# The output projections' last transposing transfers on ScalarE's queue, and another order of the FFN's raw tiles

## The chip, the cores and the metric

The kernel runs on one core of a Trainium2 chip. The metric is the device time of one execution in microseconds; 2091.7 us is the median of three runs of the kernel before (2091.61 to 2091.89). The core has TensorE (matrix products, called PE in the profile, with its weight loads as PEld), VectorE (DVE), ScalarE (ACT), GpSimd (POOL) and SyncE (SP). SP computes nothing here; its queue issues transfers. ScalarE and GpSimd can issue transfers too, from the same queue as their other instructions, in order.

## The reference

Two decoder layers over a residual stream of 256 positions by 2048 columns, in float32. Each layer mixes, projects, and then runs a gated FFN:

```python
for layer in range(DEPTH):                    # DEPTH = 2
    xn = rms_norm(h, norm_mix[layer])
    if layer % 2 == 0:                        # window attention beside an mLSTM
        mix = swa_mlstm_mixer(xn, w_in_even[j], w_out_even[j], ...)
    else:                                     # forgetting attention
        mix = forgetting_attention_mixer(xn, w_in_odd[j], fox_b_f[j], w_out_odd[j])
    h = h + mix                               # mix ends with a 2048 x 2048 output projection
    h = h + swiglu(rms_norm(h, norm_ffn[layer]), w_gate[layer], w_up[layer], w_down[layer])
return rms_norm(h, norm_final)

def swiglu(xn, w_gate, w_up, w_down):         # hidden width 5632
    return (jax.nn.silu(xn @ w_gate) * (xn @ w_up)) @ w_down
```

## The kernel before

**Products.** Every float32 operand is split into a high part of fewer bits (`hi`, written by ScalarE as a cast, L206 for plain chunks and L380 elsewhere) and the rest (`lo`, a subtraction on VectorE, L207 and L381). A product is three matmuls, hi by hi, hi by lo and lo by hi, summed in PSUM (`three`, L557 to L559; in `gemm` L244 to L246). Weights come in chunks of 256 rows by 512 columns, 512 KB, loaded by the SP queue into raw tiles (L145). Four raw tiles (pool `wr`) serve the plain chunks. The split parts of a plain chunk go into one of six `hi` tiles of the pool `wp`.

**The output projection.** `out_proj` makes the 2048 columns in four blocks `n` of 512, two at a time: blocks 0 and 1, then 2 and 3. When a block is done, VectorE adds it to the residual `h` (`add_out`, L395, one instruction for each half of the positions), ScalarE takes sums of squares for the norm (`square_sum`, L267), and the block has to be turned so that its columns lie on the partitions for the FFN's products. `split_turned` does this with transfers: ScalarE copies the block's two 16-bit planes (L338, two copies), and for each plane and each half of the positions one transposing transfer (L340) moves it, four for a block. SP issues them, in its one queue with the weight loads. A function `join` comes back: ScalarE merges the planes (L345), then scales and splits the result into `xh`, `xl` (L386, L387), and for the mixed pairs makes sums and differences (L326, L294 to L297, into `sx`).

**When the joins run.** The joins of blocks 0 and 1 run inside the second half of the projection. Those of blocks 2 and 3 run in the FFN's first group, at its steps 3 and 5 (`LATER = (6, 10, 3, 5)`, `run_due`), each ordered behind ScalarE's latest cast. Step p of the group needs the columns 256 p to 256 p + 255 of the turned input: steps 0 to 3 those of blocks 0 and 1, steps 4 and 5 those of block 2, steps 6 and 7 those of block 3.

**The FFN's steps.** `pair_group` walks eight steps (`ORDER`: plain at 0, 2, 4, 6 and 7, mixed at 1, 3 and 5). A plain step takes a gate chunk and an up chunk, 24 matmuls. A mixed step makes the same products with seven instead of eight block products, 21 matmuls. It loads both chunks into one raw tile of four pieces from the list `quads`, casts three pieces at once (L380, 128x1536), lets VectorE form differences in place (L645, L648, L649), and casts those into two `hi` tiles (L380, two casts of 128x1024).

**The raw tiles of the mixed steps.** `quads` has three tiles, used in turn. `own` is the sixth tile of `wp`, free when a chunk of the projection is done with. The other two are the slots of the tag `quad` in the FFN's pool; one of them was the room in which block 1 was turned (`scrap`), the other is unused before the FFN. After the projection the other five tiles of `wp` are the `stock` for the FFN's split parts.

**What sets the order.** The kernel's text gives the order of work. A planner goes through it, holds each instruction until by its own estimates its inputs are ready, and so writes one fixed order for each engine's queue; a queue is then worked off strictly in order, an instruction waiting at its head for semaphores. A transfer's issue counts as an instruction of the queue that issues it. `issue_after` puts an instruction behind another one on its engine.

Of the kernel before, what the change touches and what calls it, by code (L numbers as in the profile page):

```python
# [7 lines left out]
F32 = mybir.dt.float32  # L8
# [9 lines left out]
P = 128  # L18
# [5 lines left out]
NB = 512  # L24
CK = 2
# [27 lines left out]
LATER = (6, 10, 3, 5)  # L53
LATER_DOWN = (5, 6)
QUADS = 2
# [13 lines left out]
def mixed_of(order):  # L69
    return [p for w, p in order if w]  # L70
# [5 lines left out]
def trunk(  # L76
# [19 lines left out]
    nc = tc.nc  # L96
# [7 lines left out]
    stock, triples, quads = [], [], []  # L104
# [110 lines left out]
    def new_acc():  # L215
        return two_banks(0, "acc")
# [8 lines left out]
    def gemm(acc, lhs, w, c0, n, k_from, k_to, k_all, skew=1, step=0, halved=False):  # L225
        k0 = k_from
        while k0 < k_to:
            last = k_to == k_all and k0 + skew * CK >= k_all
            chunks = [load_chunk(w, kc, c0, n) for kc in range(k0, k_all if last else k0 + CK, CK)]
            run_due(later, step + k0 // CK)  # L230
            order = [(i, t) for i in range(len(chunks) * CK) for t in range(NT)]
            if last:
                order.sort(key=lambda it: it[1])
            order = [(i, t, slice(0, n)) for i, t in order]
            if last and halved:
                m = CK * (len(chunks) * NT - 1)
                order = order[:m] + [(i, t, slice(a, a + n // 2)) for a in (0, n // 2) for i, t, _ in order[m:]]
            for i, t, cs in order:
                k = k0 + i
                hi, lo = (c[:, i % CK, cs] for c in chunks[i // CK])  # L240
                ah, al = lhs(k)
                ts = slice(t * P, (t + 1) * P)
                o = acc[t][:, cs]
                nc.tensor.matmul(o, ah[:, ts], hi, start=(k == 0), stop=False)  # L244
                nc.tensor.matmul(o, ah[:, ts], lo, start=False, stop=False)  # L245
                nc.tensor.matmul(o, al[:, ts], hi, start=False, stop=(k == k_all - 1 and cs.stop == n))  # L246
            k0 += len(chunks) * CK
# [14 lines left out]
    def square_sum(key, n):  # L262
        if n == 0:
            sums[key] = sm.tile([P, NT, 4], F32, tag="ss", name="ss")
        for t in range(NT):
            junk = junk_of[0].tile([P, NB], BF16, tag=junk_of[1], name="junk", bufs=junk_of[2])
            nc.scalar.activation(  # L267
                junk, h[:, t, n * NB : (n + 1) * NB], AF.Square, accum_out=sums[key][:, t, n : n + 1]
            )
# [34 lines left out]
    def split_scaled(idx, n, extra=None, joined=None):  # L304
        both = two_banks(1, "pt") if joined is None else None
        for half in range(2):
            if joined is None:
                pt = both[half].rearrange("p (i t q) -> p i t q", i=2, t=NT)
                for i in range(2):
                    k = 4 * n + 2 * half + i  # L310
                    for t in range(NT):
                        nc.tensor.transpose(pt[:, i, t, :], h[:, t, k * P : (k + 1) * P], ident)
            else:
                pt = joined[:, 2 * half : 2 * half + 2, :].rearrange("p i (t q) -> p i t q", t=NT)
            for i in range(2):
                k = 4 * n + 2 * half + i
                src = pt[:, i, :, :].rearrange("p t q -> p (t q)")
                split_gained(xh[:, k, :], xl[:, k, :], src, idx * KT + k)
            pair = 2 * n + half
            if extra is not None and (pair in mixed_of(ORDER) or pair == FOURTH):  # L320
                sh, sl, x4, pool = extra

                def copies(full):
                    for i in range(2):
                        g = gT[:, idx * KT + 2 * pair + i : idx * KT + 2 * pair + i + 1]
                        nc.scalar.mul(full[:, i, :], pt[:, i, :, :].rearrange("p t q -> p (t q)"), g)  # L326

                if pair == FOURTH:
                    sums_of(pool, rooms(xh), rooms(xl), copies, x4=x4)
                else:  # L330
                    j = mixed_of(ORDER).index(pair)
                    sums_of(pool, sh[:, j, :, :], sl[:, j, :, :], copies)

    def split_turned(idx, n, flat, turned, extra=None):
        planes = flat.bitcast(U16).rearrange("p (b t n) -> p b t n", b=2, t=NT)
        hu = h[:, :, n * NB : (n + 1) * NB].bitcast(U16).rearrange("p t (n b) -> p t n b", b=2)
        for b in range(2):
            nc.scalar.copy(planes[:, b, :, :], hu[:, :, :, b])  # L338
            for t in range(NT):
                nc.sync.dma_start_transpose(turned[:, b, :, t, :], planes[:, b, t, :])  # L340

        def join():
            ju = flat.bitcast(U16).rearrange("p (n b) -> p n b", b=2)
            for b in range(2):
                nc.scalar.copy(ju[:, :, b], turned[:, b, :, :, :].rearrange("p k t q -> p (k t q)"))  # L345
            split_scaled(idx, n, extra, flat.rearrange("p (k s) -> p k s", k=4))

        return join
# [18 lines left out]
    def scrap(fp, n):  # L367
        if n % 2 == 0:
            box = fp.tile([P, 4, NB], F32, tag="c", name="box", bufs=1)
            halves = box[:, 0:2, :], box[:, 2:4, :]  # L370
        elif n == 3:
            halves = [fp.tile([P, 3, NB], F32, tag=f"sd{i}", name="box", bufs=1)[:, 0:CK, :] for i in range(2)]
        else:
            box = fp.tile([P, 2 * CK, NB], F32, tag="quad", name="box", bufs=QUADS)
            halves = box[:, 0:2, :], box[:, 2:4, :]
        flat, turned = (a.rearrange("p a n -> p (a n)") for a in halves)
        return flat, turned.bitcast(U16).rearrange("p (b k t q) -> p b k t q", b=2, t=NT, q=P)
# [14 lines left out]
    def add_out(acc, n):  # L392
        for t in range(NT):
            o = h[:, t, n * NB : (n + 1) * NB]
            nc.vector.tensor_tensor(out=o, in0=acc[t], in1=o, op=ALU.add)  # L395
# [139 lines left out]
    def out_proj(w, idx, key, extra):  # L535
        last, rest = KT - 4, []
        for n0 in (0, 2):
            accs = [new_acc() for _ in range(2)]
            for i in range(2):
                gemm(accs[i], m_of, w, (n0 + i) * NB, NB, 0, last, KT, step=6 * i)  # L540
            for i in range(2):
                gemm(accs[i], m_of, w, (n0 + i) * NB, NB, last, KT, KT, step=6)
                add_out(accs[i], n0 + i)
                (later if n0 == 0 else rest).append(
                    (LATER[n0 + i], split_turned(idx, n0 + i, *scrap(extra[3], n0 + i), extra))
                )
                square_sum(key, n0 + i)
        return rest
# [247 lines left out]
    def close_layer(layer, w_out, idx, key, **rest):  # L796
        with tc.tile_pool(name=f"fp{layer}", bufs=2) as fp:
            junk_of[:] = fp, "tmp", 2
            nx = len(mixed_of(ORDER))
            nd = max(len(mixed_of(o)) for o in DOWN.values())  # L800
            sx = [fp.tile([P, nx, 4, P], F32R, name=f"sx{i}", bufs=1) for i in range(2)]
            x4 = fp.tile([P, 2, P], F32R, name="x4", bufs=1)
            todo = out_proj(w_out, idx, key, (*sx, x4, fp))
            sd = [fp.tile([P, nd, 4, P], F32R, tag=f"sd{i}", name=f"sd{i}", bufs=1) for i in range(2)]
            triples.extend([fp.tile([P, 3, NB], F32R, name=f"{a}{i}", bufs=1) for a in ("hi", "lo")] for i in range(2))
            stock.extend([slot() for _ in range(5)])
            own = wp.tile([P, 2, CK, NB], F32R, tag="hi", name="raw").rearrange("p a k n -> p (a k) n").bitcast(F32)
            quads.extend([own] + [fp.tile([P, 2 * CK, NB], F32, tag="quad", name="raw", bufs=QUADS) for _ in range(QUADS)])
            ffn(layer, fp, sx, x4, sd, key, todo, **rest)
            stock.clear()  # L810
            triples.clear()
            quads.clear()
# [380 lines left out]
    with tc.tile_pool(name="od", bufs=1) as od:  # L1193
# [80 lines left out]
        for i in range(4):  # L1274
# [23 lines left out]
            elif i < 3:  # L1298
                n = NB if i == 1 else VT
                vs.append(nat1(project(wi1, c_v + (i + 1) * NB, n), n, "vn", bufs=2))  # L1300

            def v_of(j, b, i=i, vn=vs[i]):
# [6 lines left out]
                lambda j, b, qt=qt: qt[:, j, b * P : (b + 1) * P],  # L1309
# [10 lines left out]
                turned=i in (0, 2),  # L1320
# [11 lines left out]
    def finish(acc, n, gf):  # L1332
        for t in range(NT):
# [31 lines left out]
            nc.scalar.dma_start(ov[:, t, NB : 2 * NB], b1)  # L1365

    close_layer(1, w_out_odd[0], 3, "f1", finish=finish)


# [47 lines left out]
```

## Time and profile before

| | |
|---|---|
| median of three runs | 2091.7 us |
| profiled execution, its own time | 2090.63 us |
| span of its instructions | 2088.8 us |
| granted TensorE clock over the span | 0.998 |
| TensorE busy | 2072.2 us |
| VectorE busy | 1806.2 us |
| ScalarE busy | 1368.3 us |
| transposing transfers of `split_turned` | 36, all issued by SP |
| output projection ends, FFN starts on TensorE | 323.1 us (layer 0), 1388.2 us (layer 1) |

The rows below are of five kinds. The page's rows give an engine's busy time, its share of the span and its number of instructions. A row of the busy times by window has the stretch, its length, the busy time and count of PE, PEld, DVE, ACT and POOL, then the granted clock, the share of time that the DMA engines were busy, and GB/s. A row of a timeline has the start in us from the span's start, the length in us, the engine (SPq and ACTq are queues that issue), line, operation, what is written and read, the shape, the count where equal neighbours were merged, and in brackets the idle time before it and what ended it. A row of waits has who waited for whom, us in total, times, and the longest. A row of one line's instructions has the minimum, median and maximum in ns. TensorE's rows show 0.39 us for a matmul, but consecutive ones start 0.23 us apart.

### The profile page before, as it was taken

Reading aid. Unit: us, or ns where it says so; the run is one execution under the profiler, and the core shown is the slowest. Engines: PE = TensorE matmul, PEld = TensorE weight load, DVE = VectorE, ACT = ScalarE, POOL = GpSimd, SP = SyncE. Lnnn points to the kernel's source line nnn. Section 1 sums busy time; section 2 is a strip of 40 time slices with the busy share of each in tenths; the row PEclk is TensorE's granted clock in tenths of the full one; section 3 lists DMA queues with packets and bytes.
Section 4 is the critical chain, followed back from the end, with each engine's and each line's share of the span. In section 5 each row is a group of like instructions: output and inputs, shape, how many; then the busy total and the mean of one; then the engine's idle time right before and its main releaser. Section 6 shows DMA issues by size and latency. Waiting matters only on the chain.

```text
span 2088.8 us, 26467 instructions
## 1 busy us (share of the span) xinstructions
PE 2072.2 (99%) x9473; PEld 1715.1 (82%) x9473; DVE 1806.2 (86%) x2169; ACT 1368.3 (66%) x1649; POOL 44.1 (2%) x69
## 2 busy tenths in 40 slices
PE   9999999999999999999999999999999999999998
PEld 7878887888888888888888888878888888888887
DVE  6788767999999989998899688679989999999984
ACT  6777677665577646667677676577655667556763
POOL 1010000000000000000000001000000000000000
PEclk9999999999999999999999999999999999999999
DMA  8566577766677666666676776586756766666754
GB/s 292 175 206 195 189 240 195 236 205 197 206 216 229 211 193 223 219 209 185 204 205 214 223 202 183 156 255 217 237 186 196 232 197 217 226 206 200 235 157 159
DMA packets 309571, 434.84 MB, mean 208 GB/s; under 512 B 106412, under 2 KB 114624, under 8 KB 309312
## 3 DMA queue, kind: packets, MB, share of 16 engines
q1 hardware_dynamic: 307088, 426.27, 65.3%
q0 software_dynamic: 1632, 5.80, 0.9%
q8 instruction: 74, 1.21, 0.2%
q10 hardware_dynamic: 720, 1.09, 0.1%
q14 instruction: 57, 0.47, 0.1%
HBM read 408.68 MB, written 2.12 MB: 197 GB/s over the span
## 4 chain that ended last, share of the span: by engine, by line
PE 91%; ACT 3%; DMA 2%; DVE 2%; issue 1%; SPq 0%; POOL 0%; POOLq 0%; ACTq 0%; DVEq 0%
PE acc L558 21%; PE acc L557 20%; PE acc L559 20%; PE prod L557 5%; PE prod L558 5%; PE prod L559 5%; PE acc L245 4%; PE acc L244 4%; PE acc L246 4%; PE p L411 1%; ACT box L345 1%; DMA box<-box 1%; DVE hi L207 1%; PE po L512 0%; DMA raw<-in_w_up_dram 0%
## 5 line engine op out<-in xcount | busy, mean ns | idle before, releaser
L206 ACT CAST hi<-raw 128x1024 fp32r<-128x1024 f32 (+3 forms) x561 | 568.2, 1025 | 361.6 <-PE acc L559 194.3
L207 DVE TENSOR_TENSOR hi<-raw,hi 128x1024 fp32r<-128x1024 f32 (+3 forms) x561 | 659.4, 1188 | 129.2 <-ACT hi L206 127.1
L559 PE MATMUL acc<-hi,xl 128*128 128x512 f32 x1320 | 512.4, 390 | 0.0
L557 PE MATMUL acc<-hi,xh 128*128 128x512 f32 x1320 | 495.8, 391 | 4.8 <-ACT hi L206 4.5
L380 ACT CAST hi<-raw 128x1024 fp32r<-128x1024 f32 (+2 forms) x299 | 345.8, 1170 | 230.4 <-PE acc L559 195.1
L558 PE MATMUL acc<-hi,xh 128*128 128x512 f32 x1254 | 487.7, 390 | 0.4 <-DVE hi L207 0.4
L557 PEld LDWEIGHTS acc<-hi,xh 128*128 128x128 f32 x1320 | 247.5, 188 | 58.7 <-ACT hi L206 6.2
L559 PEld LDWEIGHTS acc<-hi,xl 128*128 128x128 f32 x1320 | 247.9, 188 | 51.7
L558 PEld LDWEIGHTS acc<-hi,xh 128*128 128x128 f32 x1254 | 235.5, 188 | 49.9 <-DVE hi L207 0.8
L381 DVE TENSOR_TENSOR hi<-raw,hi 128x1024 fp32r<-128x1024 f32 (+1 forms) x204 | 241.2, 1183 | 10.1 <-ACT hi L380 9.3
L381 DVE TENSOR_TENSOR lo<-raw,hi 128x1536 fp32r<-128x1536 f32 x95 | 166.8, 1755 | 48.1 <-ACT hi L380 46.0
L559 PE MATMUL acc<-hi,ml 128*128 128x512 f32 x466 | 181.0, 389 | 0.0
L557 PE MATMUL acc<-hi,mh 128*128 128x512 f32 x466 | 173.2, 389 | 0.0
L558 PE MATMUL acc<-hi,mh 128*128 128x512 f32 x437 | 170.4, 390 | 0.1
L245 PE MATMUL acc<-hi,mh 128*128 128x512 f32 (+1 forms) x322 | 126.3, 392 | 0.0
L244 PE MATMUL acc<-hi,mh 128*128 128x512 f32 (+1 forms) x322 | 125.8, 391 | 0.0
L246 PE MATMUL acc<-hi,ml 128*128 128x512 f32 (+1 forms) x322 | 123.7, 391 | 0.0
L645 DVE TENSOR_TENSOR raw<-raw 128x1024 f32<-128x1024 f32 x95 | 115.8, 1219 | 0.3
L557 PEld LDWEIGHTS acc<-hi,mh 128*128 128x128 f32 x466 | 87.5, 188 | 18.2
L559 PEld LDWEIGHTS acc<-hi,ml 128*128 128x128 f32 x466 | 87.5, 188 | 18.1
L245 PE MATMUL acc<-hi,xh 128*128 128x512 f32 (+3 forms) x288 | 99.9, 347 | 0.2 <-DVE hi L207 0.2
L246 PE MATMUL acc<-hi,xl 128*128 128x512 f32 (+3 forms) x288 | 99.1, 345 | 0.0
(364 smaller groups left out, 3077.8 us busy)
## 6 DMA issues: line engine op xcount, KB each, us to landing
raw<-in_w_gate_dram SPq DMA_DIRECT2D x176, 512.0 KB, 4.3
raw<-in_w_up_dram SPq DMA_DIRECT2D x176, 512.0 KB, 4.8
raw<-in_w_down_dram SPq DMA_DIRECT2D x176, 512.0 KB, 4.7
raw<-in_w_in_odd_dram SPq DMA_DIRECT2D x88, 512.0 KB, 5.1
raw<-in_w_in_even_dram SPq DMA_DIRECT2D x51, 512.0 KB, 4.8
raw<-in_w_out_even_dram SPq DMA_DIRECT2D x32, 512.0 KB, 5.0
raw<-in_w_out_odd_dram SPq DMA_DIRECT2D x32, 512.0 KB, 4.8
hr<-in_w_in_even_dram SPq DMA_DIRECT2D x12, 512.0 KB, 4.4
```

The source lines that it names most:

```text
L206: latest[0] = nc.scalar.copy(hi[:, k, 0:n], raw[:, k, 0:n])
L207: nc.vector.tensor_tensor(out=lo[:, k, 0:n], in0=raw[:, k, 0:n], in1=hi[:, k, 0:n].bitcast(F32), op=ALU.subtract)
L244: nc.tensor.matmul(o, ah[:, ts], hi, start=(k == 0), stop=False)
L245: nc.tensor.matmul(o, ah[:, ts], lo, start=False, stop=False)
L246: nc.tensor.matmul(o, al[:, ts], hi, start=False, stop=(k == k_all - 1 and cs.stop == n))
L345: nc.scalar.copy(ju[:, :, b], turned[:, b, :, :, :].rearrange("p k t q -> p (k t q)"))
L380: cast = nc.scalar.copy(dst_h, src)
L381: nc.vector.tensor_tensor(out=dst_l, in0=src, in1=dst_h.bitcast(F32), op=ALU.subtract)
L557: nc.tensor.matmul(o, ah, hi, start=start, stop=False)
L558: nc.tensor.matmul(o, ah, lo, start=False, stop=False)
L559: nc.tensor.matmul(o, al, hi, start=False, stop=stop)
L645: nc.vector.tensor_tensor(out=raw[:, 1:4:2, :], in0=raw[:, 3:4, :].broadcast_to([P, 2, NB]), in1=raw[:, 1:3, :], op=ALU.subtract)
```

## The change

The four transposing transfers of a block are issued on a queue that the caller names. `out_proj` names ScalarE's queue for blocks 2 and 3 and SP's for blocks 0 and 1; the FFN's own call of `split_turned` keeps SP. So eight transfers a layer, 16 in all, move from SP's queue to ScalarE's, where they stand behind the plane copies in program order. The list `quads` begins with the first of the two slots of the tag `quad`, `own` comes second, the other slot third. Nothing else is changed, but the planner works out all queues anew.

```diff
-    def split_turned(idx, n, flat, turned, extra=None):
+    def split_turned(idx, n, flat, turned, extra=None, queue=nc.sync):
...
             for t in range(NT):
-                nc.sync.dma_start_transpose(turned[:, b, :, t, :], planes[:, b, t, :])
+                queue.dma_start_transpose(turned[:, b, :, t, :], planes[:, b, t, :])
...
                 (later if n0 == 0 else rest).append(
-                    (LATER[n0 + i], split_turned(idx, n0 + i, *scrap(extra[3], n0 + i), extra))
+                    (LATER[n0 + i], split_turned(idx, n0 + i, *scrap(extra[3], n0 + i), extra, nc.scalar if n0 else nc.sync))
                 )
...
-            quads.extend([own] + [fp.tile([P, 2 * CK, NB], F32, tag="quad", name="raw", bufs=QUADS) for _ in range(QUADS)])
+            quads.extend(fp.tile([P, 2 * CK, NB], F32, tag="quad", name="raw", bufs=QUADS) for _ in range(QUADS))
+            quads.insert(1, own)
```

## The prediction

> **What bounds the kernel now.** I read the page first, then the busy times by window, then the timelines of TensorE, ScalarE, VectorE and the SP queue around the two places where TensorE is not full.
>
> ```profile
> span 2088.8 us, 26467 instructions
> PE 2072.2 (99%) x9473; PEld 1715.1 (82%) x9473; DVE 1806.2 (86%) x2169; ACT 1368.3 (66%) x1649; POOL 44.1 (2%) x69
> ...
> 280.00:323.00 43.00, 43.00 (x191) 35.59 (x191) 29.17 (x40) 33.18 (x47) 0.00 (x0) 1.00 0.81 255
> 323.00:345.00 22.00, 18.13 (x70) 13.57 (x69) 12.97 (x20) 16.14 (x24) 0.69 (x1) 0.92 0.71 129
> 345.00:420.00 75.00, 74.85 (x327) 60.65 (x326) 73.98 (x85) 53.91 (x59) 0.00 (x0) 1.00 0.76 239
> ...
> 1387.00:1410.00 23.00, 20.43 (x88) 15.95 (x87) 16.74 (x23) 19.61 (x27) 0.71 (x1) 1.00 0.67 170
> 1410.00:1500.00 90.00, 89.82 (x394) 73.35 (x393) 88.80 (x101) 63.65 (x70) 0.00 (x0) 1.00 0.69 218
> ```
>
> The last three numbers of a window's row are the granted clock, the DMA share and GB/s. TensorE is busy 99% of the span, so a change away from its holes can give nothing. The change acts where an output projection hands over to its FFN: 323 to 345 us in layer 0, 1387 to 1410 us in layer 1. There TensorE misses 22.00 - 18.13 = 3.87 us, and about 8% of 22 us, 1.76 us, to a granted clock of 0.92; in layer 1 it misses 23.00 - 20.43 = 2.57 us at full clock. So 5.6 + 2.6 = 8.2 us is all that the change can win.
>
> ```profile
> 314.87 1.06 ACT L206 CAST hi<-raw 128x1024 fp32r<-128x1024 f32 x1 [3.25 <-DMA raw<-in_w_gate_dram]
> 317.04 1.06 ACT L206 CAST hi<-raw 128x1024 fp32r<-128x1024 f32 x1 [1.12 <-DMA raw<-in_w_up_dram]
> 320.04 0.64 ACT L267 ACTIVATE junk<-h 128x512 bf16<-128x512 f32 x1 [1.94 <-DVE h L395]
> ...
> 320.68 1.98 ACT L338 COPY box<-h 128x1024 uint16<-128x1024 uint16 x2
> ...
> 326.50 1.48 ACT L380 CAST hi<-raw 128x1536 fp32r<-128x1536 f32 x1 [3.22 <-DMA raw<-in_w_up_dram]
> ...
> 331.25 2.56 ACT L345 COPY box<-box 128x1024 uint16<-128x1024 uint16 x2 [2.65 <-DMA box<-box]
> 333.67 1.98 ACT L338 COPY box<-h 128x1024 uint16<-128x1024 uint16 x2
> ...
> 336.18 1.03 ACT L206 CAST hi<-raw 128x1024 fp32r<-128x1024 f32 x1
> 337.11 1.04 ACT L380 CAST hi<-raw 128x1024 fp32r<-128x1024 f32 x1
> 338.06 1.71 ACT L386 ACTIVATE xh<-box,gT 128x256 fp32r<-128x256 f32 x4
> ...
> 340.48 1.03 ACT L380 CAST hi<-raw 128x1024 fp32r<-128x1024 f32 x1
> 341.42 1.05 ACT L206 CAST hi<-raw 128x1024 fp32r<-128x1024 f32 x1
> 342.37 2.43 ACT L380 CAST hi<-raw 128x1536 fp32r<-128x1536 f32 x2
> 344.70 2.58 ACT L345 COPY box<-box 128x1024 uint16<-128x1024 uint16 x2
> ...
> 348.61 1.05 ACT L206 CAST hi<-raw 128x1024 fp32r<-128x1024 f32 x1
> ```
>
> This is ScalarE in layer 0. The plain casts L206 name the FFN's even steps: two for step 0 (314.87, 317.04), two for step 2 (336.18, 341.42), the first of step 4 at 348.61. From 331.25 ScalarE has no gap. What TensorE stands for at the end is step 2's first cast:
>
> ```profile
> 337.26 0.73 PE L557 MATMUL acc<-hi,xh 128*128 128x512 f32 x2 [2.14 <-ACT hi L206]
> ```
>
> So the slow matmuls and the small waits before it are hidden by this wait: had TensorE been quicker, it would have stood longer. The hole is set by ScalarE's queue, and I cost the change on that queue.
>
> Why is the queue late? The first mixed pair (step 1) is in the tile `own`, and it is the last one loaded:
>
> ```profile
> 292.85 0.82 SPq L145 DMA_DIRECT2D raw<-in_w_gate_dram  x1
> ...
> 317.21 0.88 SPq L145 DMA_DIRECT2D raw<-in_w_gate_dram  x2
> 318.14 1.62 SPq L145 DMA_DIRECT2D raw<-in_w_up_dram  x2
> 321.73 18.12 SPq L340 DMA_TRANSPOSE box<-box  x8
> 339.95 3.37 SPq L145 DMA_DIRECT2D raw<-in_w_gate_dram  x2
> ...
> SPq L340 <- ACT box L338: 10.9, 2, 8.0
> ...
> 317.10 0.68 DVE L649 TENSOR_TENSOR raw<-raw 128x512 f32<-128x512 f32 x1
> ...
> 328.01 1.76 DVE L381 TENSOR_TENSOR lo<-raw,hi 128x1536 fp32r<-128x1536 f32 x1 [5.37 <-ACT hi L380]
> 329.68 0.68 DVE L395 TENSOR_TENSOR h<-acc,h 128x512 f32<-128x512 f32 x1
> ```
>
> The load of 292.85 fills the free raw tile, and by the old order that is the second mixed pair's (step 3); VectorE ends its additions at 317.78. `own` is loaded by the second of the two at 317.21 and by the first at 318.14, and its cast waits until 326.50. Behind it VectorE waits 5.37 us, and the residual addition of the last block (329.68) stands behind that; so the last block's plane copies come at 333.67, and the SP queue, which issues its transposes, stands for them 8.0 us.
>
> **The change part by part.** I follow ScalarE from 320.04 to the end of step 4's first cast, 349.66.
>
> *Order of the raw tiles.* The tile loaded at 292.85 now serves step 1. Its first cast and additions are over before 318, so its two last casts (337.11 and 340.48, 0.95 us each to the next start) can go into the gaps of 3.25, 1.12 and 1.94 us ahead of 320, if a `hi` slot is free there. That takes 1.9 us off the stretch (0 if no slot is free). The wait for `own` (3.22 us) moves to step 3, 10 us of TensorE work later, and its place is filled. It also gives TensorE a whole step 1 to work on, 9 matmuls at the 0.23 us of two rows further down more than now.
>
> *The transposes.* Eight issues a layer leave SP and stand in ScalarE's queue. SP's own gain I put at nothing: behind its transposes the next load, at 339.95, goes into a raw tile that step 2's chunk leaves, which is cast at 336.18 only, and the lower half is formed after that; without this cover it would be 8.0 us of late loads. What ScalarE pays:
>
> ```profile
> L340 SPq DMA_TRANSPOSE box<-box x36: 1190/1263/1713, 280.3 to 1400.5; - x36
> ...
> 2079.97 0.71 ACT L1364 ACTIVATE h<-h,ft 128x512 f32<-128x512 f32 x1
> 2080.10 0.34 ACTq L1361 DMA_DIRECT2D out_dram<-h  x1
> ...
> 2079.86 0.36 SPq L1359 DMA_DIRECT2D out_dram<-h  x1
> ...
> 323.11 0.39 PE L557 MATMUL acc<-hi,xh 128*128 128x512 f32 x1
> 323.33 0.39 PE L558 MATMUL acc<-hi,xh 128*128 128x512 f32 x1
> ```
>
> No row has a transpose issued by ScalarE. The same plain transfer takes 0.36 us to issue on SP and 0.34 on ScalarE, so I take the transpose at SP's median, 1.26 us; the lower bound is 0.34. The issue at 2080.10 runs beside an activation dispatched before it, but what stands behind it must wait. So 8 x 1.26 = 10.1 us, less two times 0.94 us, when the first plane's transposes run beside the second plane's copy: 8.2 us (bounds 0 to 10.1). Queued behind them are the residual's square sums, step 2's casts, `own`'s cast and the joins; VectorE and then TensorE wait for these.
>
> The Trainium skill, "DMA: Bandwidth & Descriptors", section "Issuing engines are not separate DMA queues", says that issuing from several engines saves only sequencer time, "usually small relative to the DMA itself". By that the transposes would be nearly free on ScalarE and the time that of the faster rival below; the row of L340 has 1.26 us an issue, against 0.34 for a plain one, and does not bear out "small".
>
> *Waits that go.* ScalarE's 3.22 and 2.65 us are filled: -5.87 us. In layer 1 the two are smaller:
>
> ```profile
> 1389.82 1.48 ACT L380 CAST hi<-raw 128x1536 fp32r<-128x1536 f32 x1 [2.16 <-DMA raw<-in_w_up_dram]
> ...
> 1393.15 2.58 ACT L345 COPY box<-box 128x1024 uint16<-128x1024 uint16 x2 [1.23 <-DMA box<-box]
> ```
>
> that is -3.39 us.
>
> *Work that may fall behind.* Ahead of 348.61 ScalarE now does the last block's join (344.70, 2.45 us to the next start) and step 5's cast (one of the two at 342.37, 1.38 us). Both belong to later steps; with the transposes later they may fall behind the cast. Bounds 0 and -3.83 us; I take the middle, -1.9.
>
> Sum, layer 0: -1.9 + 8.2 - 5.87 - 1.9 = -1.5 us. Layer 1: -1.9 + 8.2 - 3.39 - 1.9 = +1.0 us. TensorE follows one for one as long as it stands for ScalarE, so -0.5 us in all. The profiled execution took 2090.63 us (its span is 2088.8, 1.8 lie around it): 2090.1. The median of the runs shown is 2091.7, 1.1 above it, so the forecast there is 2091.2 us: no change.
>
> **The rivals.** *Faster: the issues hardly hold ScalarE, or the casts go ahead of them.* If an issue costs ScalarE 0.34 us as its plain ones do, 8 of them are 2.7 us, and the sums become -7.0 and -4.5 us; if the planner puts step 2's casts ahead of the last block's four transposes, 5.0 us leave the stretch, -6.5 and -4.0 us. Either is more than the holes hold: -5.6 - 2.6 = -8.2 us, 2083.5 us. For it speaks that `own`, the cause of the late addition, is out of the way; against it, that the joins and copies that remain fill ScalarE from 331.25 on.
>
> *Slower: ScalarE stands at a transpose.* Transfers share a few completion counters, so an issue can stand until an earlier load has landed (one issue of 1.713 us in the row above). On SP that delays loads alone; on ScalarE it delays every cast. `own`'s load of 318.14 let its cast start at 326.50, 8.4 us later. If `own` gets only the slot that the projection's last chunk leaves at 323.1, it lands at 331.5, and the last block's transposes, ready at about 327.7 (two copies after the first block's four issues), stand 3.8 us. Twice that on top of the sum is +7.1 us: 2098.8 us. It decides as soon as `own` is loaded later than 327.7 - 8.4 = 319.3 us. Against it: now it goes out at 317.6.
>
> *The swap does nothing:* the planner already took the early tile for whatever is ready. Then step 1's parts stay at 337 and the sum is +3.3 us: 2095.0, still within the bound.
>
> **How the numbers follow.** About 0.2%, 4.2 us, is what a measurement of this kernel can tell from no change: 2087.5 to 2095.9. The forecast with the swap's failure has 0.47; its own range, with the unknown term at its ends in both layers and the swap at 0, is 2087.4 to 2095.0. The faster rival has 0.30 (2083.5 to 2087.5), the slower one 0.23 (2095.9 to 2099). The range that holds 8 in 10 reaches into both: 2083.5 to 2099.
>
> **What the changed profile would show.** The transposes L340 after 320 us stand on ScalarE's queue, each near 1.26 us; if they are near 0.34 the faster rival is right. The first 128x1536 cast after 305 is followed by its two 128x1024 casts ahead of 320; if they stay at 337, the swap did nothing. The residual addition of the last block comes at 324 instead of 329.68. TensorE's hole before step 2 shrinks in layer 0 and grows in layer 1. Wrong is all of it if ScalarE is not gapless after 331, or if a new wait of SP or VectorE ends last there.

## The result, and the profile after

| | median | runs | range |
|---|---|---|---|
| before | 2091.8 us | 4 | 2091.61 to 2092.78 |
| after | 2107.95 us | 4 | 2105.66 to 2108.59 |

The ratio is 1.0074, with an interval of 1.0057 to 1.0092: the change makes the kernel 16 us slower; the range forecast ended 7 us above the kernel before. Of the executions of the kernel before that were measured beside e1 to e4 below, two took 2504.77 and 5229.55 us, far above all others, and are left out of every median. The profiled execution of the changed kernel took 2105.66 us. Its page begins:

```profile
span 2103.9 us, 26467 instructions
...
PE 2074.9 (99%) x9473; PEld 1717.9 (82%) x9473; DVE 1806.8 (86%) x2169; ACT 1366.8 (65%) x1649; POOL 45.5 (2%) x69
```

The instructions are as many as before and VectorE and ScalarE are as long busy; 15 us of span have been added in which they stand. The busy times by window say where (after the stretch and its length: PE, PEld, DVE, ACT, POOL, then the granted clock):

```profile
323.00:345.00 22.00, 18.42 (x80) 14.59 (x79) 10.47 (x12) 15.03 (x19) 0.69 (x1) 1.00 0.79 205
345.00:365.00 20.00, 17.41 (x61) 13.34 (x62) 20.00 (x29) 15.58 (x24) 0.00 (x0) 0.83 0.46 147
365.00:385.00 20.00, 17.71 (x69) 13.60 (x69) 16.47 (x24) 10.14 (x12) 0.00 (x0) 0.91 0.59 193
...
1387.00:1410.00 23.00, 23.00 (x104) 19.03 (x103) 10.58 (x14) 13.46 (x19) 0.70 (x1) 1.00 0.97 268
1410.00:1430.00 20.00, 13.64 (x52) 10.29 (x51) 19.60 (x26) 18.69 (x25) 0.00 (x0) 0.91 0.25 62
1430.00:1450.00 20.00, 17.22 (x71) 12.73 (x70) 16.73 (x24) 11.68 (x15) 0.00 (x0) 1.00 0.62 206
```

In layer 1, whose FFN now starts at 1394.8 us, the hole of before is gone (23.00 of 23 us against 20.43), and a larger one stands behind it: 6.4 us missing from 1410 to 1430, 2.8 us in the next 20. In layer 0 the hole lies at 341 instead of 335, and two windows with a clock of 0.83 and 0.91 follow. The waits of TensorE and its timeline name what it stands for:

```profile
PE acc L557 <- ACT xh L386: 10.1, 2, 5.0
```

```profile
341.39 0.39 PE L559 MATMUL acc<-hi,sx 128*128 128x512 f32 x1
346.81 0.80 PE L557 MATMUL acc<-hi,xh 128*128 128x512 f32 x1 [5.03 <-ACT xh L386]
```

Once a layer TensorE comes to step 4 and stands 5 us for block 2's join, for which the prediction's sum has no term. Behind it matmuls start 0.43 us apart instead of 0.23 for some 5 us; the granted clock is 0.50 from 347 to 350 us, and so 0.83 over the window. But TensorE comes to step 4 early. In the kernel before it began it later, at 349.69:

```profile
349.69 0.62 PE L557 MATMUL acc<-hi,xh 128*128 128x512 f32 x2
```

So in layer 0 the time is lost behind the first 5 us stand and not by it alone: by 385 us the changed kernel has 209 matmuls behind it since 323 us, the kernel before 243. ScalarE's timeline shows why the join is late:

```profile
318.36 2.00 ACT L380 CAST hi<-raw 128x1024 fp32r<-128x1024 f32 x2
...
323.18 1.28 ACTq L340 DMA_TRANSPOSE box<-box  x1
...
324.49 1.47 ACTq L340 DMA_TRANSPOSE box<-box  x1
...
324.63 1.03 ACT L206 CAST hi<-raw 128x1024 fp32r<-128x1024 f32 x1
326.05 3.19 ACTq L340 DMA_TRANSPOSE box<-box  x2
329.34 2.00 ACT L338 COPY box<-h 128x1024 uint16<-128x1024 uint16 x2 [3.68 <-issue]
...
334.19 2.56 ACTq L340 DMA_TRANSPOSE box<-box  x2
336.80 1.48 ACT L380 CAST hi<-raw 128x1536 fp32r<-128x1536 f32 x1 [3.29 <-issue]
338.18 2.56 ACT L345 COPY box<-box 128x1024 uint16<-128x1024 uint16 x2
340.60 1.04 ACT L206 CAST hi<-raw 128x1024 fp32r<-128x1024 f32 x1
341.55 1.46 ACT L380 CAST hi<-raw 128x1536 fp32r<-128x1536 f32 x1
342.92 2.53 ACT L345 COPY box<-box 128x1024 uint16<-128x1024 uint16 x2
345.32 1.03 ACT L206 CAST hi<-raw 128x1024 fp32r<-128x1024 f32 x1
346.25 1.70 ACT L386 ACTIVATE xh<-box,gT 128x256 fp32r<-128x256 f32 x4
```

The eight issues come in two blocks, 12.1 us long in all, and twice ScalarE does nothing but issue: 3.68 and 3.29 us. Block 2's L345 starts at 338.18 (331.25 before), and between it and the L386 that TensorE needs stand a cast of the third pair, block 3's L345 and both casts of step 4. L386 comes at 346.25; before it came at 338.06. The swap itself did as meant: step 1's two last casts stand at 318.36. `own` is loaded by the SP queue from 324.19 on:

```profile
324.19 0.42 SPq L145 DMA_DIRECT2D raw<-in_w_gate_dram  x1
```

The experiments come back to VectorE's waits from 318 to 385 us, before

```profile
DVE lo L381 <- ACT hi L380: 5.4, 1, 5.4
DVE tot L273 <- ACT junk L267: 3.4, 1, 3.4
```

and after:

```profile
DVE hi L207 <- ACT hi L206: 6.5, 5, 3.2
DVE tot L273 <- ACT junk L267: 5.1, 1, 5.1
DVE lo L381 <- ACT hi L380: 3.5, 1, 3.5
```

### The profile page after: what moved, and what is told of

Same layout as the page of the kernel before. It is cut to its first block, busy times and chain, and to the rows that moved or that the text cites. A ratio compares the mean times of both kernels' runs of the same rounds, so it can differ in the third digit from the quotient of the medians.

```text
span 2103.9 us, 26467 instructions
## 1 busy us (share of the span) xinstructions
PE 2074.9 (99%) x9473; PEld 1717.9 (82%) x9473; DVE 1806.8 (86%) x2169; ACT 1366.8 (65%) x1649; POOL 45.5 (2%) x69
## 5 line engine op out<-in xcount | busy, mean ns | idle before, releaser
L557 PE MATMUL acc<-hi,xh 128*128 128x512 f32 x1320 | 498.8, 393 | 15.8 <-ACT xh L386 10.1
L380 ACT CAST hi<-raw 128x1024 fp32r<-128x1024 f32 (+2 forms) x299 | 344.8, 1168 | 222.6 <-PE acc L559 190.7
L381 DVE TENSOR_TENSOR hi<-raw,hi 128x1024 fp32r<-128x1024 f32 (+1 forms) x204 | 241.3, 1185 | 13.1 <-ACT hi L380 12.3
L381 DVE TENSOR_TENSOR lo<-raw,hi 128x1536 fp32r<-128x1536 f32 x95 | 166.9, 1756 | 46.6 <-ACT hi L380 44.5
```

The source lines that it names most:

```text
L380: cast = nc.scalar.copy(dst_h, src)
L381: nc.vector.tensor_tensor(out=dst_l, in0=src, in1=dst_h.bitcast(F32), op=ALU.subtract)
L557: nc.tensor.matmul(o, ah, hi, start=start, stop=False)
```

## The experiments

Theory A says that the issues' time in ScalarE's queue is the cost, theory B that it is the swap, theory C that it is only the new order of joins and casts. Medians stand against the kernel before as measured beside each group of runs, whose median was 2091.3 to 2092.5 us; ratios have 95% intervals.

**One part at a time.** The swap alone, the transposes alone, and the swap with one block's transposes:

```diff
-    (LATER[n0 + i], split_turned(..., extra, nc.scalar if n0 else nc.sync))
+    (LATER[n0 + i], split_turned(..., extra))
```


> All transposes are issued by SP again, the new order of the raw tiles stays. Theory A (the eight issues in ScalarE's queue, 12.1 us a layer in the profile of after, push block 2's join from 338.06 to 346.25, and TensorE stands 5 us a layer for it): the join's L386 comes at 335 to 339, TensorE does not stand at 341, time 2086 to 2093 us. Theory B (the new order of the raw tiles, with `own` loaded at 324 instead of 317, costs the time): 2104 to 2109 us. Theory C (only the planner's order: joins placed behind the casts of steps 3 and 4): here too block 2's join stands behind `own`'s cast and step 4's first cast, so TensorE stands 3 to 5 us at step 4, 2100 to 2108 us.

```diff
-            quads.extend(fp.tile(...) for _ in range(QUADS))
-            quads.insert(1, own)
+            quads.extend([own] + [fp.tile(...) for _ in range(QUADS)])
```


> The eight transposes a layer stay on ScalarE's queue, the raw tiles have their old order. A: the issues stay and `own` is late again for step 1; 2104 to 2114 us, L386 of block 2 at 343 or later. B: as before, 2090 to 2094 us. C: the planner puts block 2's join ahead of the casts of steps 3 and 4 here, so TensorE does not stand for it; 2090 to 2097 us.

```diff
-    (LATER[n0 + i], split_turned(..., extra, nc.scalar if n0 else nc.sync))
+    (LATER[n0 + i], split_turned(..., extra, nc.scalar if n0 + i == 3 else nc.sync))
```


> New order of the raw tiles; block 2's four transposes go back to SP, only block 3's four stay on ScalarE, all four ahead of block 2's join. A: about half of the 12.1 us leaves ScalarE's queue, L386 of block 2 comes at 339 to 342, TensorE's stand of 5 us a layer is gone or below 1 us; 2088 to 2097 us. B: 2104 to 2109 us. C: order nearly as in after but with L386 ahead of block 3's join, 2098 to 2105 us.

```diff
-    (LATER[n0 + i], split_turned(..., extra, nc.scalar if n0 else nc.sync))
+    (LATER[n0 + i], split_turned(..., extra, nc.scalar if n0 + i == 2 else nc.sync))
```


> New order of the raw tiles; only block 2's four transposes stay on ScalarE, block 3's four go back to SP. The order of ScalarE's casts and joins is nearly that of after, without block 3's issues, which took 6.2 us there (1.50, 2.14, 1.23, 1.29). A: L386 of block 2 comes about 6 us earlier, at 340, and the stand of 5 us a layer goes; 2090 to 2098 us. B and C: as after, 2104 to 2109 us.

| kernel | median us | ratio |
|---|---|---|
| e1 swap alone | 2091.38 | 0.9997 (0.9988 to 1.0006) |
| e2 transposes alone | 2096.6 | 1.0023 (1.0012 to 1.0034) |
| e3 swap, block 3's transposes | 2098.5 | 1.0035 (1.0021 to 1.0048) |
| e4 swap, block 2's transposes | 2098.63 | 1.0034 (1.0021 to 1.0047) |

B falls: the swap alone costs nothing, and wins nothing. The transposes alone cost 4.6 us, not the 12 and more that A asked for; on top of the swap they cost some 17, each half of them 7. So the two parts are not a sum. A met e1, missed e2 widely, and e3 and e4 by 1.5 and 0.6 us; C met e2 and e3 and missed e1 and e4.

What the swap gives is taken back in e1's layer 0 at step 3: TensorE runs full up to it and stands for the cast of `own`, whose second load SP issues only behind its eight transposes. In the changed kernel both loads are out by 324.66.

```profile
334.25 0.58 SPq L145 DMA_DIRECT2D raw<-in_w_up_dram  x1
...
340.45 0.50 PE L557 MATMUL prod<-hi,xh 128*128 128x512 f32 x1 [2.40 <-ACT hi L380]
```

In e2 ScalarE's timeline shows why eight issues can be cheap:

```profile
326.98 1.99 ACT L338 COPY box<-h 128x1024 uint16<-128x1024 uint16 x2 [4.36 <-issue]
...
330.12 1.45 ACT L380 CAST hi<-raw 128x1536 fp32r<-128x1536 f32 x1
330.98 1.21 ACTq L340 DMA_TRANSPOSE box<-box  x1
331.48 1.35 ACT L345 COPY box<-box 128x1024 uint16<-128x1024 uint16 x1
...
336.22 1.04 ACT L380 CAST hi<-raw 128x1024 fp32r<-128x1024 f32 x1 [1.24 <-issue]
```

The first stand lies where ScalarE waited for `own` before (3.22 us); the second block is issued from 330.98 on beside the cast of 330.12 and the two copies and a cast behind it, and only 1.24 us stick out. In e4 TensorE still stands for the join (9.6 us in all), though half the issues are gone:

```profile
342.66 2.52 ACT L345 COPY box<-box 128x1024 uint16<-128x1024 uint16 x2 [2.51 <-DMA box<-box]
...
345.99 1.70 ACT L386 ACTIVATE xh<-box,gT 128x256 fp32r<-128x256 f32 x4
```

There block 2's L386 stands behind block 3's L345, which waits for transposes that SP issues late. That spoke for the order, and the next four runs changed it.

**Other due times for the joins.** `LATER` is (6, 10, 3, 5); e5 and e6 edit the changed kernel, e7 and e8 the swap alone:

```diff
-LATER = (6, 10, 3, 5)
+LATER = (6, 10, 3, 6)
```


> The changed kernel with block 3's join due at step 6 instead of 5 (LATER 6, 10, 3, 6): the eight issues stay on ScalarE, and block 3's L345 (2.4 us) no longer stands between block 2's L345 and its L386. Theory A (the issues take ScalarE's time, ahead of everything): only those 2.4 us are won, L386 of block 2 at 343.8, TensorE still stands 2.5 us a layer at step 4: 2099 to 2105 us. Theory C (the delay is the order: block 2's join behind block 3's): TensorE's stand for xh goes, 2090 to 2096 us. Theory B (the swap) is out by the swap alone (2091.4 us).

```diff
-LATER = (6, 10, 3, 5)
+LATER = (6, 10, 2, 6)
```


> The changed kernel with block 2's join due at step 2 and block 3's at step 6 (LATER 6, 10, 2, 6): behind the eight issues ScalarE does block 2's L345 first, then `own`'s cast, step 4's gate cast, the third pair's cast, then L386 of block 2. A: 2.4 + 0.95 us leave the way to L386, which comes at 342.9; TensorE stands 1.5 us or a little more, and the casts of steps 2 and 3 stay behind the issues: 2096 to 2103 us. C: no stand, 2090 to 2096 us.

```diff
-LATER = (6, 10, 3, 5)
+LATER = (6, 10, 2, 5)
```


> The swap alone (all transposes on SP) with block 2's join due at step 2: block 2's L345 no longer stands behind block 3's, which stood 4.16 us for its transposes there. A: no issue on ScalarE and the join early: L386 of block 2 at 333 to 337; the stand of 2.6 us at 337.7 and the slow matmuls after it shrink: 2084 to 2091 us. C: the same or better, 2083 to 2088 us. If neither, a wait for step 3 (`own`'s cast, which comes behind the joins here) takes its place: 2091 to 2095 us.

```diff
-LATER = (6, 10, 3, 5)
+LATER = (6, 10, 2, 6)
```


> As the run before, with block 3's join due at step 6 as well (LATER 6, 10, 2, 6), so that `own`'s cast and step 4's casts stand behind block 2's join alone. A and C: 2082 to 2090 us, best of all if step 3's casts are what TensorE waits for; a wait at step 6 for block 3's L386, which now comes late, would give 2092 to 2098 us.

None of the theories holds in any of the four: 2107.38 us (1.0073, 1.0059 to 1.0087), 2106.05 (1.0066, 1.0053 to 1.0079), 2097.45 (1.0024, 1.0015 to 1.0033) and 2096.14 (1.0019, 1.0011 to 1.0028). Only e8's time lies in a range that was named beside the theories (2092 to 2098 us, for a wait at step 6), but TensorE waits for L386 there no more than 1.9 us in both layers, and 5.3 us for the casts L380. In e6 the wait for the join is gone from the list of TensorE's waits, and others have its place: 8.3 us for the casts L380 and 7.1 us for the subtractions L381. The wait named last is not the cause: whatever is put first, something else comes late. C falls.

**What bounds the group.** Theory E says VectorE, because it has no gap from 337 to 372 us in the kernel before; F says ScalarE. The subtractions or the casts of four chunks a layer were done twice, and the mixed steps' differences of the first group moved to GpSimd, in the kernel before and in the swap alone:

```diff
+AGAIN = (1, 0)
...
-    latest = [None]
+    latest, again = [None], [0, 0]
...
-            latest[0] = nc.scalar.copy(hi[:, k, 0:n], raw[:, k, 0:n])
-            nc.vector.tensor_tensor(
+            for _ in range(1 + again[1]):
+                latest[0] = nc.scalar.copy(hi[:, k, 0:n], raw[:, k, 0:n])
+            for _ in range(1 + again[0]):
+                nc.vector.tensor_tensor(
...
-        begun = set()
+        begun, opening = set(), halves is None and len(todo) == 2
...
+                    again[:] = AGAIN if opening and pos in (4, 6) else (0, 0)
                     hi, lo = load_chunk(w, k0, c0, NB)
+                    again[:] = 0, 0
```


> The kernel before, with VectorE's subtraction for the plain chunks of steps 4 and 6 of each layer's first FFN group done twice (four more of 1.14 us a layer, 9.1 us in all; the result is the same). Theory E: VectorE is what bounds the first group (it has no gap from 337 to 372 us in the kernel before), and each us it idles or works more is paid by TensorE; the swap won nothing because of this, and the issues on ScalarE cost what they make VectorE idle. E: 2098 to 2103 us. Rival F: ScalarE's queue, gapless from 331 to 362 us, is the bound: 2091 to 2095 us.

```diff
+AGAIN = (0, 1)
```


> The kernel before, with ScalarE's casts of the same four chunks a layer done twice (four more of 0.95 us a layer, 7.6 us in all; the result is the same). E: VectorE works on beside them, 2091 to 2096 us. F: 2098 to 2101 us.

The third edit uses `opening` as defined above; e12 is the same on the swap alone.

```diff
+                diff = nc.gpsimd if opening else nc.vector
-                nc.vector.tensor_tensor(
+                diff.tensor_tensor(
...
-                nc.vector.tensor_tensor(out=raw[:, 2, :], in0=raw[:, 2, :], in1=raw[:, 1, :], op=ALU.subtract)
-                nc.vector.tensor_tensor(out=raw[:, 0, :], in0=raw[:, 0, :], in1=raw[:, 2, :], op=ALU.subtract)
+                diff.tensor_tensor(out=raw[:, 2, :], in0=raw[:, 2, :], in1=raw[:, 1, :], op=ALU.subtract)
+                diff.tensor_tensor(out=raw[:, 0, :], in0=raw[:, 0, :], in1=raw[:, 2, :], op=ALU.subtract)
```


> The kernel before, with the three differences of each mixed step of the first group (L645, L648, L649: 1.14 + 0.6 + 0.6 us, three steps a layer, 7 us a layer) on GpSimd instead of VectorE. E: VectorE has 14 us less to do in the two groups; 3 to 9 us are won, 2083 to 2089 us. F: 2090 to 2094 us. If GpSimd needs far longer for one than VectorE, the second casts of the mixed steps come late and it is slower than before.

> The swap alone (all transposes on SP) with the same differences on GpSimd. E: with VectorE relieved, what the swap gives TensorE early is no longer taken back at step 4: faster than the run before and than the swap alone, 2080 to 2087 us. F: as the swap alone, 2090 to 2093 us.

e9 took 2100.26 us (1.0039, 1.0026 to 1.0051): 7.8 of the 9.1 us are paid, as E said. e10 took 2104.41 us (1.0055, 1.0041 to 1.0068), 11.9 us for 7.6 us of casts, against E as it stood and more than F asked for. These casts are also what VectorE's subtractions wait for, so that e10 does not tell ScalarE's time from VectorE's waiting. The relief failed, 2102.02 us (1.0047, 1.0034 to 1.0059) and 2100.65 us (1.004, 1.0027 to 1.0053), and decides nothing, since GpSimd slows VectorE (below).

**Less ScalarE work in the stretch, and issues elsewhere.** In the changed kernel, the one before and the swap alone, the square sums of blocks 2 and 3 come at step 6; and the changed kernel with blocks 0 and 1 on ScalarE's queue too:

```diff
-                square_sum(key, n0 + i)
-        return rest
+                if n0 == 0:
+                    square_sum(key, n0 + i)
+                else:
+                    rest.append((SQUARES, lambda n=n0 + i: square_sum(key, n)))
+        return sorted(rest, key=lambda d: d[0])
...
-        r = rstd(key)
+        r = None
...
+                r = rstd(key) if r is None else r
```


> The changed kernel, with the square sums of blocks 2 and 3 (L267, four a layer, 0.72 us each with their read-out, 2.9 us a layer on ScalarE) done at step 6 of the first group instead of at its beginning; the norm's factor is worked out behind the group, where it is used. Theory A' (ScalarE's time between the projection's end and step 4 is what is paid: 14.6 us of standing at issues in two layers became 16 us of time, 7.6 us of doubled casts became 12): 5.8 us of ScalarE's time leave the stretch, 2100 to 2104 us. Theory G (what is paid is the order alone, or the late loads): 2106 to 2109 us.

> The kernel before with the same square sums at step 6. A': 2085 to 2089 us, faster than both kernels. G, or if VectorE alone is the bound: 2091 to 2093 us.

> The swap alone (all transposes on SP) with the square sums at step 6. A': the swap wins only where ScalarE does not wait afterwards for `own` (loaded behind SP's transposes): 2084 to 2090 us. G: 2090 to 2093 us.

```diff
-    (LATER[n0 + i], split_turned(..., extra, nc.scalar if n0 else nc.sync))
+    (LATER[n0 + i], split_turned(..., extra, nc.scalar))
```


> The changed kernel with the eight transposes of blocks 0 and 1 on ScalarE's queue as well (16 issues a layer). These fall into the projection's second half, where ScalarE is idle for 10 of 43 us and TensorE never waits. A': an issue costs only where ScalarE is short: 2105 to 2111 us, as the changed kernel. If an issue costs its time anywhere: 16 more of about 1 us, 2118 to 2126 us.

A' is wrong in all four; G holds in e13 alone. The late squares gave 2108.54 us (1.0082, 1.0068 to 1.0096), 2095.18 (1.0021, 1.0012 to 1.0029) and 2099.65 (1.0038, 1.0024 to 1.0052). In e14 the first hole is a little smaller, 58.75 instead of 58.13 us of TensorE from 323 to 385, but the next group waits:

```profile
415.97 0.60 PE L561 MATMUL acc<-hi,xh 128*128 128x512 f32 x1 [2.42 <-ACT c L581]
```

So this test also moved a cost behind the stretch and does not speak cleanly. e16 took 2120.07 us (1.0136, 1.0122 to 1.0149), as if an issue cost its time anywhere: 16 more cost 12 us. A part of this lies in the projection, where TensorE now stands 1.5 us in the row below (all 45.00 us are busy in the changed kernel) and 1.9 us in layer 1; 6.7 us more than in the changed kernel are missing in the 62 us behind the two FFN starts:

```profile
280.00:325.00 45.00, 43.47 (x190) 35.03 (x188) 26.94 (x38) 31.29 (x43) 0.00 (x0) 1.00 0.89 232
```

**The same ScalarE time without an issue.** The plane copies of blocks 2 and 3 done three times, all transposes on SP, with the new and with the old order of the raw tiles:

```diff
-            nc.scalar.copy(planes[:, b, :, :], hu[:, :, :, b])
+            for _ in range(3 if extra is not None and n > 1 else 1):
+                nc.scalar.copy(planes[:, b, :, :], hu[:, :, :, b])
```


> The swap alone (all transposes on SP), with each of the plane copies L338 of blocks 2 and 3 done three times instead of once (the result is the same): eight more copies of 0.95 us a layer, 7.6 us, about what ScalarE stands at its eight issues in the changed kernel (6.97 and 7.60 us a layer). Theory S: an issue on ScalarE's queue is nothing but ScalarE time at that place, and with the new order of the raw tiles no wait is left there to cover it: 2102 to 2109 us, like the changed kernel. Rival: the issues cost through something of their own (loads and transposes that land late, the waits within them): 2092 to 2098 us.

> The kernel before with the same eight more copies a layer. S: here ScalarE's waits for `own` and for the turned block (5.87 us in layer 0, 3.39 in layer 1) can cover 9.3 of the 15.2 us, as they covered the issues in the run with the transposes alone: 2095 to 2101 us. If nothing covers them: 2105 to 2109 us. Rival as above: 2092 to 2094 us.

e17 took 2091.57 us (1.0002, 0.9993 to 1.0011): 15.2 us more of ScalarE work, and not a microsecond paid: 10 us below what S asked for and just below the rival's range, so S does not hold with the new order. e18 took 2095.78 us (1.002, 1.0011 to 1.0028), inside S's range, so that alone it would have spoken for S. ScalarE's timeline of e17:

```profile
331.94 1.47 ACT L381 CAST hi<-raw 128x1536 fp32r<-128x1536 f32 x1
333.31 1.04 ACT L339 COPY box<-h 128x1024 uint16<-128x1024 uint16 x1
334.26 1.48 ACT L381 CAST hi<-raw 128x1536 fp32r<-128x1536 f32 x1
335.65 1.04 ACT L339 COPY box<-h 128x1024 uint16<-128x1024 uint16 x1
```

Here the planner put four of the eight further copies in among the casts and behind the first ones: `own`'s cast (L381, 128x1536) starts at 331.94 and the third pair's at 334.26, against 336.80 and 341.55 in the changed kernel, where all eight issues stand ahead of both. Two other things differ. SP issues `own`'s loads at 322.86 and 323.27, ahead of its transposes, as the changed kernel nearly does (324.19 and 324.66) and e1 does not (the second at 334.25), so against e1 a part of the copies' cost may have been won back there. And block 3's join stands behind block 2's scaling (349.42 and 343.76); but e5 made that order in the changed kernel and won nothing. VectorE's waits from 318 to 385 us are then these, 7.9 us in all (15.4 in the changed kernel, 11.1 before, 9.1 in e1):

```profile
DVE tot L273 <- ACT junk L267: 5.1, 1, 5.1
DVE hi L207 <- ACT hi L206: 2.6, 3, 1.9
DVE hi L382 <- ACT hi L381: 0.2, 1, 0.2
```

**VectorE's time over all runs.** The busy times by window from 323 to 385 and from 1388 to 1450 us, for the kernel before,

```profile
323.00:385.00 62.00, 58.13 (x243) 46.01 (x242) 52.95 (x67) 45.70 (x58) 0.69 (x1) 0.97 0.73 205
1388.00:1450.00 62.00, 59.39 (x257) 47.58 (x256) 56.02 (x70) 46.03 (x56) 0.71 (x1) 1.00 0.66 198
```

for the changed kernel,

```profile
323.00:385.00 62.00, 53.53 (x209) 41.53 (x209) 46.94 (x63) 40.76 (x54) 0.69 (x1) 0.92 0.62 182
1388.00:1450.00 62.00, 52.86 (x219) 41.25 (x218) 45.91 (x61) 43.65 (x57) 0.70 (x1) 0.97 0.63 181
```

and for e17:

```profile
323.00:385.00 62.00, 59.42 (x248) 47.92 (x247) 54.69 (x69) 53.81 (x67) 0.69 (x1) 0.94 0.69 204
1388.00:1450.00 62.00, 58.60 (x249) 46.99 (x248) 55.87 (x70) 53.65 (x65) 0.70 (x1) 0.97 0.67 198
```

give VectorE's idle time as 124 us less the two DVE numbers: 15.0, 31.2 and 13.4 us. ScalarE is 13.1 and 10.0 us longer busy in e17 than in the changed kernel, and TensorE is better fed. TensorE's numbers give the whole of the 16 us: in the changed kernel it stands 17.6 of the 124 us instead of 6.5, and the granted clock, 0.92 and 0.97 instead of 0.97 and 1.00, is about 5 us more. The same for the kernels with VectorE's own work unchanged, beside what each took over the kernel before:

| kernel | VectorE idle of 124 us | time over before, us |
|---|---|---|
| e18 | 12.6 | +3.9 |
| e17 | 13.4 | -0.3 |
| before | 15.0 | 0 |
| e1 | 16.5 | -0.7 |
| e14 | 18.6 | +3.9 |
| e2 | 19.1 | +4.6 |
| e8 | 20.3 | +3.9 |
| e7 | 21.2 | +5.2 |
| e4 | 22.3 | +6.6 |
| e10 | 23.1 | +11.9 |
| e3 | 25.7 | +6.5 |
| e15 | 27.6 | +8.3 |
| e13 | 28.2 | +17.2 |
| after | 31.2 | +16.2 |
| e5 | 31.8 | +15.2 |
| e16 | 32.7 | +28.8 |
| e6 | 32.8 | +13.8 |

Time rises with what VectorE idles: by 16.2 us each from before to after, and most others lie within 5 us of that line; e18 and e16 are 6 and 11 us off it. This alone shows no cause. VectorE's work is the same in all these kernels, so a longer time has to appear as its idle time somewhere, and the table only says that it appears here; VectorE also waits when TensorE frees tiles late. The second window is not moved with a slower kernel either; with both windows begun at the FFN's start the changed kernel has 29.9 us instead of 31.2. What speaks on the cause is e9, where VectorE's added work is paid, and e17, where ScalarE's is not.

## Why the prediction was wrong

*What held.* Step 1's casts moved ahead of 320. An issue on ScalarE takes what it takes on SP or more, 1.39 us in the median against 1.26:

```profile
L340 SPq DMA_TRANSPOSE box<-box x20: 1195/1262/1268, 280.4 to 1361.0; - x20
L340 ACTq DMA_TRANSPOSE box<-box x16: 1206/1394/2434, 323.2 to 1406.5; - x16
```

The term of 8.2 us a layer was 6.97 us of standing in layer 0 (3.68 + 3.29); the faster rival, with 0.34 us an issue, had no place. The Trainium skill ("DMA: Bandwidth & Descriptors", "Issuing engines are not separate DMA queues") calls the sequencer's time to initiate a DMA usually small beside the DMA itself; here it is 1.39 us of a median of 3.0 us from issue to landing, which does not bear that out. With the old order of the raw tiles the sum came near as well: with no gain from the swap it was +3.3 us, and e2, which is close to that case, measured +4.6. As the sum follows the wrong point (below), this may be luck.

*The step that failed* is the one on which all terms rest: "The hole is set by ScalarE's queue, and I cost the change on that queue", with TensorE following ScalarE one for one up to the end of step 4's first cast. That point did come earlier, and by more than the forecast of -1.5 and +1.0 us. From the first square sum to its end ScalarE takes 20.2 us instead of 29.6 in layer 0 (321.49 to 341.64; before 320.04 to 349.66) and 20.8 instead of 27.2 in layer 1. By this measure 15.8 us were won, and the kernel lost 16.2. TensorE does not follow that cast: at step 4 it stands 5 us for block 2's L386, which now comes behind the cast, and where that wait is gone (e6) for other casts and subtractions. The sum followed one queue to one point, and TensorE needs what VectorE makes of ScalarE's casts as well: e17 put 15.2 us into ScalarE's queue without a loss, e9 paid 7.8 of 9.1 us on VectorE. The reading that fits these runs is that VectorE, which has no gap from 337 to 372 us in the kernel before, must work through the group's steps without a gap, and that what counts is when ScalarE hands it casts, not how full ScalarE is.

Three terms fall with this step. The swap's -1.9 us a layer was worth nothing clear of noise (e1): in layer 0 TensorE runs full to step 3 and stands there for `own`, whose load SP's transposes hold back. That also answers "SP's own gain I put at nothing": with the new order of the raw tiles `own`'s second load goes out at 324.66 instead of e1's 334.25 once the transposes have left SP. The waits filled, -5.87 and -3.39 us, were counted beside the swap, which itself takes the wait for `own` from the place where the first four issues stand; in e1 ScalarE waits only 1.27 us there. And -1.9 us for work of later steps that falls behind came true in full and won nothing: step 5's cast (341.55) and block 3's L345 (342.92) do stand behind step 4's first cast (340.60), but ahead of block 2's L386 (346.25).

The sum's own range had a slip too: its upper end of 2095.0 us puts either the swap or the unknown term at nothing; with both, as its words say, it is 2098.8 us, still 9 us short.

*The signs named.* The addition of the last block came at 326.83, not 324, behind a subtraction whose cast ScalarE did at 324.63. The hole before step 2 shrank in both layers and returned at step 4, "a new wait" as the last sentence feared, though of TensorE and not of SP or VectorE. ScalarE is not gapless after 331.

*The slower rival* was nearest, though it too stopped at 2098.8 us: its condition was met (`own` loaded at 324.2, later than 319.3), and issues grew to 2.43 us. All 16 together took 24.8 us, 4.7 more than at 1.26; it had priced 7.6 us for this. But they do not stand for a load's landing. By the trace's semaphores the longest in layer 0, 2.14 us from 331.95, takes over the counter of a load that had landed at 330.40, and the one of 2.43 us, from 1402.70, that of a load landed at 1400.95; each follows the issue before it within 0.05 us. What lengthens them stays open.

*Open.* Which step failed is shown; why the issues cost so much is not. That it is because they stand in blocks ahead of casts that VectorE needs is read from the timelines of e17 and after; a run with block 3's copies and issues moved behind `own`'s cast was not made. Why e18 pays 3.9 us with VectorE as busy as in e17, and what in e16 the issues delay inside the projection, stays open. No version tried beats the kernel before.

## What to carry to other kernels

The engine that a wait names can be the last link only and not the bound: before costing a change on its queue, look for the engine that has no gap in the stretch behind the hole, and ask what feeds it. If you follow one queue to a point, make sure that this point is what the fast engine waits for. Price an issue on a compute engine's queue by what stands behind it, block by block, and never credit one wait to two parts of a change. Where filling a hole only lets the fast engine run sooner into the next one, the gain is nothing.

## What the runs showed of the hardware

A VectorE subtraction with two inputs in SBUF slows when GpSimd works on SBUF: in e11 a 128x1024 subtraction, 1.22 us in the median, took up to 3.43 us.

```profile
344.53 3.32 POOL L646 TENSOR_TENSOR raw<-raw 128x1024 f32<-128x1024 f32 x1 [6.43 <-DVE lo L381]
```

```profile
345.50 3.43 DVE L207 TENSOR_TENSOR hi<-raw,hi 128x1024 fp32r<-128x1024 f32 x1
```

The Trainium skill, "SBUF — State Buffer", section "SBUF: two separate sides", says that the two engines share one pair of ports by an exclusive lock, held for a whole instruction; here GpSimd's subtraction of 344.53 ends at 347.85, 2.35 us after the subtraction's start at 345.50, and the subtraction is 2.21 us longer than 1.22: the trace agrees. And a queue can issue while its engine works: in e2 ScalarE issued from 330.98 to 332.19, while its cast of 330.12 still ran, and its copy of 331.48 began in the midst of that issue.
